# Hybrid encoder step on one core: another order and chaining of the 20 products of the down projection, later x tiles, later last h combinations

## The chip, the cores and the metric

The kernel runs on one core of one Trainium2 chip. The metric is the device time of one execution in microseconds (us), the median of several. Engines are named as in the profile: PE (TensorE matmul) and PEld (its weight loads), DVE (VectorE), ACT (ScalarE), POOL (GpSimd), SP (SyncE, which here only issues transfers).

## The reference

One step of a small streaming encoder with two layers, in float32, for 1024 prompt tokens and 8 x 16 sample tokens (1152 rows of 1024). Each layer is attention (a projection, banded attention, an output projection added to the residual x) and then an MLP, which is all that matters here:

```python
def mlp(x, g_norm, w_up, w_down):
    return jnp.square(jax.nn.relu(rmsnorm(x, g_norm) @ w_up)) @ w_down
...
        hp = hp + mlp(hp, g_mlp[layer], w_up[layer], w_down[layer])
        hs = hs + mlp(hs, g_mlp[layer], w_up[layer], w_down[layer])
```

`w_up` is 1024 x 4096, `w_down` 4096 x 1024. The second product, h @ w_down added to x, is called "down" below, the first "up".

## The kernel before, in words

**Stages.** For each of the two layers the kernel runs attention, the output projection, up (`mlp_up`) and down (`mlp_down`). x lives in memory as nine tiles of 128 tokens: 0 to 7 are the prompt and ST (8) is the sample. Every float32 operand of a matmul is split in a high and a low part (ACT casts, line 128; DVE subtracts, line 134), and every product of tiles is three matmuls (`mm3`, lines 746 to 748).

**Down as 20 products.** One pass covers half of the 4096 hidden columns, and there are two passes per layer (s = 0, 1). In a pass the h matrix is cut in 3 token thirds by 4 blocks, the weights in 4 blocks by 2 column halves, and the output x in 3 thirds (`PARTS`: which three x tiles form each third) by 2 column halves, six output pieces. Instead of 24 block products there are 20 (`RANK`), each of one combination of h blocks with one combination of weight blocks (`W_FORMS`, one or two blocks each: 4 of the 20 have one, 16 have two). `OUT_FORMS` says to which of the six pieces, with which sign, a product is added. A layer thus has 40 products, which I number 0 to 39 in the order in which they run.

**Chains.** `CHAINS` holds that order. The products of one chain accumulate in the same three PSUM banks (one per x tile of a third). After a product, DVE adds a bank to the x tiles wherever the form of this product differs from that of the next of the chain (line 1119, a "read": one for each differing piece and bank). A read inside a chain must be done before PE comes back to that bank in the next product; after the end of a chain the next one takes other banks. A negative number in `CHAINS` is a product of the other sign, made by swapping the two weight blocks, or, for those in `NEG_H`, by storing the negated h combination.

**What a product needs.** The h combination of a product is loaded from memory into one of three tiles a0 to a2 (`load_h`, line 1031, 768 KB) and split in place. The weight blocks are loaded once per pass into raw tiles r0 to r10 (`load_w`, 1 MB each, places by `RAW_AT`); for a form of two blocks DVE first adds or subtracts them (line 1067, here an "add"); the result is split into one of two tiles w0, w1. In the loop over products, iteration n loads the weights of product n + 3 (`AHEAD`), splits those of n + 1, adds those of n + 2, issues the matmuls and the reads of n, and then loads the h combination of the next product whose tile is free.

**One queue.** All these loads are issued by SP, and `load` chains each behind the one before, so their order on SP is the order of the program: a load that has to wait keeps back all that come after it. The x tiles are loaded on the same chain. `X_AT` says ahead of which product's h combination a third is loaded (three tiles of 512 KB): thirds 2, 1 and 0 with products 0, 1 and 3. `DOWN_HOME` lists the places of the tiles in SBUF from left to right. They lie over what up used: x5, x6, x7, the bias tiles, r4 and r5 lie over up's output tiles h, and so can be loaded only when these are read out.

**The h combinations.** Up works in 16 blocks of 256 hidden columns. After each pair of blocks DVE forms the combinations (`forms_even`, five transfers and two operations; `forms_odd`, 16 operations L935 to L968 of 128 x 384, mostly in place, and 15 transfers), and POOL stores each to memory (`form_store`, line 911, 192 KB). `COLS` says which third of an h tile is meant by which block row; it goes together with `PARTS`. The last pair of blocks feeds the second pass of down alone.

**The order on the engines** is made when the program is built: a scheduler walks the instructions by priority (program order, moved by `high_priority`) and by a model of when each can run; each engine then runs its own list strictly in order.

Of the kernel before, what the change touches and what calls it, by code (L numbers as in the profile page):

```python
# [8 lines left out]
F32 = mybir.dt.float32  # L9
# [7 lines left out]
P = 128  # L17
# [3 lines left out]
ST = NT  # L21
# [7 lines left out]
NFB = FF // FB  # L29
SIDE = (0, 1, 6, 2, 3, 4, 5)  # L30
RANK = 20
PARTS = ((5, 6, 7), (ST, 0, 1), (2, 3, 4))
COLS = (2, 0, 1)
W_FORMS = (
    "+.......", ".......+", "+......-", ".+.....+", ".....+..",
    "..+..-..", "..+.....", "...+.+..", "..+.+...", "+.....+.",
# [7 lines left out]
    "....+.", "..+.-.", "+.+...", "...-.+", "..+.-.",  # L44
)
CHAINS = (
    ((4,), (0, 10), (14, 15), (-13, 18), (12, 1, 2, 17, 9, 8), (-6, 5, 11, 3, 7), (16, 19)),
    ((0,), (-4, 15), (-14, 10), (-13, 18), (19, 16), (12, 1, 2, 17), (-6, 5, 11, 7, 3), (9, 8)),
)
NEG_H = ((6,), (6, 4))  # L50
RAW_AT = ((0, 7, 2, 8, 1, 6, 9, 3), (10, 7, 6, 3, 5, 4, 9, 8))
EPS = 1e-6
BIG = 1e30
NREL = 257
# [40 lines left out]
class Build:  # L95
# [682 lines left out]
    def mlp_up(self, layer, sx, x8, rp, raw0):  # L778
        nc = self.nc
        tt = nc.vector.tensor_tensor  # L780
        with ExitStack() as st:
# [9 lines left out]
            hp = self.pool(st, f"uh{layer}")  # L791

            def weights(b):
                raw = self.up_raw(layer, rp, b) if b else raw0
                quad = []
                for h in range(2):
                    q = [
                        take(f"q{b % 2}{v}") if h else rp[0].tile([P, 4, FB], F32R, tag=f"q{v}", name="wq")
                        for v in range(2)
                    ]  # L800
                    self.split(q[0], q[1], raw[h])
                    quad.append(q)
                b11, b12 = raw[0][:, :, 0:P], raw[0][:, :, P:FB]
                b21, b22 = raw[1][:, :, 0:P], raw[1][:, :, P:FB]
                t = b11, b22, b12, b21
                tt(t[0], b12, b11, ALU.subtract)
                tt(t[2], b22, b12, ALU.subtract)
                tt(t[1], b22, t[0], ALU.subtract)
                tt(t[3], b21, t[1], ALU.subtract)
                ts = [None] * 4  # L810
                for n in (1, 2, 0, 3):
                    w = take(f"t{b % 2}{n}")
                    self.split(w[:, 0], w[:, 1], t[n])
                    ts[n] = w[:, 0], w[:, 1]
                q = lambda h, n: [quad[h][v][:, :, n * P : n * P + P] for v in range(2)]
                return quad, [q(0, 0), q(1, 0), q(1, 1), ts[3], ts[0], ts[1], ts[2]]
# [79 lines left out]
            for b in range(NFB):  # L896
                quad, ws = weights(b)
                eh = [hp.tile([P, 3 * 3 * P], F32, tag="h", name="h", bufs=7) for _ in range(2)]
                if b == 0:
                    tokens(eh, quad, ws, slice(0, 256), False)  # L900
                    tokens(eh, quad, ws, slice(256, 512), True)
                else:
                    tokens(eh, quad, ws, slice(0, 512), True)
                if b % 2 == 0:
                    even = eh
                    self.forms_even(b // 2, eh)
                else:
                    self.forms_odd(b // 2, even + eh, hp.tile([P, 3 * 3 * P], F32, tag="h", name="ht", bufs=7))

    def form_store(self, c):  # L910
        return lambda p, z: self.nc.gpsimd.dma_start(self.hd[c // 4][:, p, c % 4], z)  # L911
# [1 line left out]
    def form_cut(self, t):  # L913
        return [t[:, COLS[i] * 3 * P : (COLS[i] + 1) * 3 * P] for i in range(3)]

# [12 lines left out]
    def forms_odd(self, c, eh, extra):  # L928
        tt, put = self.nc.vector.tensor_tensor, self.form_store(c)
        add, sub = ALU.add, ALU.subtract  # L930
        (a0, s10, a8), (a1, a5, s11), (a2, a6, a10), (a3, a7, a11) = map(self.form_cut, eh)
        u, w, z = self.form_cut(extra)
        put(16, a6)
        put(8, a2)
        tt(a8, a6, a8, add)  # L935
        put(14, a8)
        tt(a10, a6, a10, add)
        put(15, a10)
        tt(u, a8, s10, sub)
        if c < 4:  # L940
            tt(w, a10, a8, sub)
        else:
            tt(w, a8, a10, sub)
        tt(z, a1, a2, sub)
        tt(a1, a1, s11, sub)
        put(7, a1)
        put(19, a11)
        tt(a7, a7, a11, add)
        put(17, a7)
        tt(a5, a5, a11, sub)  # L950
        put(12, a5)
        tt(a2, z, s11, sub)
        put(5, a2)
        if c < 4:
            tt(w, a2, w, add)
        else:
            tt(w, w, a2, sub)
        put(4, w)
        tt(z, a5, z, sub)
        put(6, z)  # L960
        tt(a6, a0, a3, sub)
        tt(a6, a6, a5, sub)
        put(1, a6)
        tt(a3, a3, a7, sub)
        put(9, a3)
        tt(a0, a0, a3, sub)
        put(2, a0)
        tt(u, a0, u, add)  # L968
        put(0, u)

    def mlp_down(self, layer, out):
# [3 lines left out]
        with ExitStack() as st:  # L975
# [11 lines left out]
            def take(tag):  # L987
                return slots.pop(tag) if tag in slots else fresh(tag)
# [38 lines left out]
            def slot(n):  # L1027
                return 1 + n % 2 if n >= total - TAIL else n % 3

            def load(dst, src):  # L1030
                a = nc.sync.dma_start(dst, src)
                if self.sp is not None:
                    self.behind(self.sp, a)
                self.sp = a

            def load_w(n):
                s, p, g, *_, raws = seq[n]
                for r, f in enumerate(W_FORMS[p]):
                    if f != "." and r not in raws:
                        raws[r] = take(f"r{RAW_AT[s][r]}")  # L1040
                        l, h = divmod(r, 2)
                        load(raws[r], wd[l // 2, l % 2][:, 4 * s : 4 * s + 4, N[h]])

            def load_h(n):
                s, p, *_ = seq[n]
                aa[n] = take(f"a{slot(n)}")
                load(aa[n][:, 1].bitcast(F32), self.hd[s][:, p])
# [3 lines left out]
            def add_w(n):  # L1051
                if n >= total:
                    return
                s, p, g, *_, raws = seq[n]
                used = [(r, f) for r, f in enumerate(W_FORMS[p]) if f != "."]
                g = g if p not in NEG_H[s] else 1
                x, y = (raws[used[i][0]] for i in (0, -1))
                if len(used) == 1:
                    assert g == 1
                    src[n] = x  # L1060
                    return
                src[n] = x if n >= total - TAIL + 2 else take(f"s{n % 2}")
                plus = used[1][1] == "+"
                assert g == 1 or not plus
                if g < 0:
                    x, y = y, x
                tt(src[n], x, y, ALU.add if plus else ALU.subtract)  # L1067

            def split_w(n):
                if n >= total:  # L1070
                    return
                w = ws[n] = take(f"w{n % 2}")
                self.split(w[:, 0], w[:, 1], src.pop(n))
                a = aa[n]
                self.split(a[:, 0], a[:, 1], a[:, 1].bitcast(F32))
# [3 lines left out]
            def early(n):  # L1079
                return self.tc.high_priority(EARLY[n]) if n < len(EARLY) else nullcontext()  # L1080

            def load_x(i):
                for t in PARTS[i]:
                    load(xs[t], self.xd[t])

            for n in range(AHEAD):
                with early(n):
                    load_w(n)
                    load_h(n)
                if n in X_AT:  # L1090
                    load_x(X_AT[n])
            add_w(0)
            split_w(0)
            add_w(1)
            for n, (s, p, g, first, final, reads, _) in enumerate(seq):
                if layer == 0 and n == RANK:
                    self.prep_bias(self.dp)
                if n + AHEAD < total:
                    load_w(n + AHEAD)
                if n + AHEAD in X_AT:  # L1100
                    load_x(X_AT[n + AHEAD])
                split_w(n + 1)
# [4 lines left out]
                for i in range(3):  # L1107
# [9 lines left out]
                    for o, v in reads:  # L1117
                        x = xs[PARTS[o // 2][i]][:, N[o % 2]]
                        tt(x, x, banks[i], ALU.add if v > 0 else ALU.subtract)  # L1119
                    for part in {o // 2 for o, _ in reads}:  # L1120
                        if last[part] == n:
                            t = PARTS[part][i]
                            nc.sync.dma_start(out(t), xs[t])
# [634 lines left out]
def make_plan(tail, second):  # L1758
# [16 lines left out]
AFTER = mybir.DependencyInfo(mybir.DependencyClass.NoSync, mybir.DependencyReason.DATA)  # L1775
EARLY = (300, 150, 110, 90)
DOWN_HOME = (
    "s0", "s1", "r0", "r1", "r2", "r3", "x5", "x6", "x7", "bias", "r4", "r5", "+384", "x2", "x3", "x0", "+640",
    "a0", "x4", "x1", "x8", "r6", "a1", "a2", "w0", "w1", "r7", "r8", "r9", "r10",
)  # L1780
TAIL = 6
AHEAD = 3
X_AT = {0: 2, 1: 1, 3: 0}
WO_ORDER = [[0, 4, 1, 5, 2, 6, 7, 3, ST], [0, 4, 1, 5, 6, 2, 7, 3, ST]]

CFG = [
# [49 lines left out]
```

## Time and profile before

| | |
|---|---|
| median of 3 runs | 2397.39 us (2394.85 to 2402.23) |
| the profiled execution, its own time | 2401.58 us |
| its span, first to last instruction | 2399.8 us, so 1.8 us lie around it |
| granted TensorE clock, mean | 0.988 |
| busy: DVE, ACT, POOL | 1787.2 us (74%), 1272.6 us (53%), 573.2 us (24%) |
| down of layer 0, first to last matmul | 805.3 to 1167 us |
| down of layer 1 | 2045.1 to 2395.4 us |

Every row of a timeline has the start, the duration, the engine, the line, the operation, out<-in and a count; in brackets stands how long the engine had been idle and who released it. In a table by windows each engine's busy time is followed by its count of instructions, and PEclk is the granted clock as a share of full speed.

### The profile page before, as it was taken

What the parts mean: (1) busy time and instruction counts of PE and PEld (TensorE: products, weight loads), DVE (VectorE), ACT (ScalarE), POOL (GpSimd) and SP (SyncE); (2) the same over time, 40 slices, a digit from 0 to 9 for tenths busy, and PEclk for the clock granted to TensorE, in tenths of its full rate; (3) what the DMA queues carried; (4) which work ended last, traced back from release to release, by engine and by line L of the source; (5) the groups of instructions that cost most, each with busy time, mean ns of one, the idle gap of its engine ahead of it and who ended that gap; (6) DMA issues with size and microseconds to landing.
All of it is one profiled execution on the core that took longest, in us unless ns stands there. A gap on an engine that the chain in (4) does not pass through costs nothing.

```text
span 2399.8 us, 33255 instructions
## 1 busy us (share of the span) xinstructions
PE 2291.6 (95%) x11429; PEld 1903.1 (79%) x11429; DVE 1787.2 (74%) x3192; ACT 1272.6 (53%) x2503; POOL 573.2 (24%) x892
## 2 busy tenths in 40 slices
PE   7998999899999889999999999998999999899998
PEld 6787877788888668877778788886888888688877
DVE  6788786666566689899567876887665664898995
ACT  3777674555555334444267666665555555344432
POOL 4334332222222100001233444444122321100000
PEclk9999999999999999999999999999999999999999
DMA  7335545244343672535543655555343444734533
GB/s 254 119 109 167 170 149 201 87 135 143 127 141 120 253 244 93 206 132 182 181 152 113 197 162 170 172 165 166 96 142 118 157 140 148 276 110 139 199 102 122
DMA packets 216377, 375.38 MB, mean 156 GB/s; under 512 B 51144, under 2 KB 125840, under 8 KB 216208
## 3 DMA queue, kind: packets, MB, share of 16 engines
q1 hardware_dynamic: 193136, 300.89, 38.9%
q0 software_dynamic: 21776, 67.65, 7.7%
q10 hardware_dynamic: 1296, 4.72, 0.5%
q8 instruction: 90, 1.47, 0.3%
q14 instruction: 79, 0.65, 0.1%
HBM read 241.23 MB, written 130.90 MB: 155 GB/s over the span
## 4 chain that ended last, share of the span: by engine, by line
PE 68%; DVE 14%; DMA 8%; issue 4%; ACT 3%; POOL 1%; SPq 1%; ACTq 0%; DVEq 0%; POOLq 0%
PE ps_x L746 5%; PE ps_x L748 5%; PE ps_x L747 5%; PE ps_c L748 5%; PE ps_c L746 5%; PE ps_c L747 5%; PE ps_mm L219 4%; PE ps_mm L217 4%; PE ps_mm L218 4%; PE ps_y L748 2%; PE ps_y L747 2%; PE ps_y L746 2%; DVE w L134 2%; PE ps_tr L324 2%; DVE x L1119 2%
## 5 line engine op out<-in xcount | busy, mean ns | idle before, releaser
L746 PE MATMUL ps_c<-w,a 128*128 128x512 f32 x960 | 380.3, 396 | 29.7 <-ACT a L128 15.9
L747 PE MATMUL ps_c<-w,a 128*128 128x512 f32 x960 | 378.9, 395 | 5.2 <-DVE w L134 5.2
L748 PE MATMUL ps_c<-w,a 128*128 128x512 f32 x960 | 378.8, 395 | 4.7 <-DVE a L134 4.5
L911 POOL DMA_DIRECT2D hd<-h x272 | 147.2, 541 | 600.6 <-ACT h L820 263.1
L128 ACT CAST a<-a 128x1536 fp32r<-128x1536 f32 x80 | 118.6, 1482 | 242.5 <-DMA a<-hd 240.1
L746 PEld LDWEIGHTS ps_c<-w,a 128*128 128x128 f32 x960 | 183.0, 191 | 75.5 <-ACT a L128 18.0
L748 PEld LDWEIGHTS ps_c<-w,a 128*128 128x128 f32 x960 | 182.8, 190 | 46.9 <-DVE a L134 8.5
L747 PEld LDWEIGHTS ps_c<-w,a 128*128 128x128 f32 x960 | 182.9, 191 | 44.0 <-DVE w L134 6.6
L1119 DVE TENSOR_TENSOR x<-x,ps_c 128x512 f32<-128x512 f32 x246 | 161.0, 679 | 31.8 <-PE ps_c L748 31.6
L134 DVE TENSOR_TENSOR a<-a 128x1536 fp32r<-128x1536 f32 x80 | 140.4, 1755 | 56.0 <-ACT a L128 56.0
L217 PE MATMUL ps_mm<-w,hh 128*128 128x512 f32 x432 | 173.2, 402 | 6.4 <-POOL w L185 2.1
L128 ACT CAST w<-s 128x2048 fp32r<-128x2048 f32 x56 | 107.2, 1914 | 126.7 <-PE ps_c L748 119.0
L219 PE MATMUL ps_mm<-w,hl 128*128 128x512 f32 x432 | 172.6, 401 | 0.8 <-DMA hl<-hTd 0.6
L218 PE MATMUL ps_mm<-w,hh 128*128 128x512 f32 x432 | 171.7, 398 | 1.6 <-DVE w L190 1.6
L746 PE MATMUL ps_x<-sx,w 128*128 128x512 f32 (+1 forms) x408 | 158.4, 388 | 3.7 <-ACT h L867 2.7
L747 PE MATMUL ps_x<-sx,w 128*128 128x512 f32 (+1 forms) x408 | 154.8, 379 | 0.0
L748 PE MATMUL ps_x<-sx,w 128*128 128x512 f32 (+1 forms) x408 | 154.8, 379 | 0.0
L128 ACT CAST w<-ru 128x512 fp32r<-128x512 f32 (+1 forms) x160 | 110.0, 708 | 84.4 <-PE ps_y L747 32.0
L134 DVE TENSOR_TENSOR ptl<-ps_tr,pth 128x512 fp32r<-128x512 f32 x180 | 122.4, 685 | 24.3 <-ACT pth L128 19.2
L134 DVE TENSOR_TENSOR w<-s,w 128x2048 fp32r<-128x2048 f32 x56 | 127.9, 2284 | 15.5 <-ACT w L128 15.5
L134 DVE TENSOR_TENSOR w<-ru,w 128x512 fp32r<-128x512 f32 (+1 forms) x160 | 126.7, 794 | 15.1 <-ACT w L128 15.0
L1067 DVE TENSOR_TENSOR s<-r,r 128x2048 f32<-128x2048 f32 x56 | 127.7, 2284 | 2.8 <-DMA r<-in_w_down 2.8
(280 smaller groups left out, 5903.3 us busy)
## 6 DMA issues: line engine op xcount, KB each, us to landing
a<-hd SPq DMA_DIRECT2D x80, 768.0 KB, 4.2
hd<-h POOLq DMA_DIRECT2D x272, 192.0 KB, 2.5
ru<-in_w_up SPq DMA_DIRECT2D x64, 512.0 KB, 3.9
r<-in_w_down SPq DMA_DIRECT2D x32, 1024.0 KB, 8.0
x<-xd SPq DMA_DIRECT2D x41, 512.0 KB, 6.3
o<-oTd SPq DMA_DIRECT2D x52, 256.0 KB, 4.3
xd<-xo SPq DMA_DIRECT2D x18, 512.0 KB, 2.8
xo<-xd SPq DMA_DIRECT2D x18, 512.0 KB, 3.9
```

The costliest lines, as they stand in the source:

```text
L128: a = nc.scalar.copy(hi, src)
L134: return a, e.tensor_tensor(lo, src, hi.bitcast(F32), ALU.subtract)
L217: nc.tensor.matmul(ps, a, w[:, 0, k, :], start=(k == 0), stop=False)
L218: nc.tensor.matmul(ps, a, w[:, 1, k, :], start=False, stop=False)
L219: self.lp = nc.tensor.matmul(ps, b, w[:, 0, k, :], start=False, stop=(k == KC - 1))
L324: self.lp = nc.tensor.transpose(pt[:, i, :], get(i), self.ident)
L746: a = mm(ps, ah, bh, start=first, stop=False, skip_group_check=True)
L747: mm(ps, ah, bl, start=False, stop=False, skip_group_check=True)
L748: return a, mm(ps, al, bh, start=False, stop=last, skip_group_check=True)
L911: return lambda p, z: self.nc.gpsimd.dma_start(self.hd[c // 4][:, p, c % 4], z)
L1067: tt(src[n], x, y, ALU.add if plus else ALU.subtract)
L1119: tt(x, x, banks[i], ALU.add if v > 0 else ALU.subtract)
```

## The change

1. `CHAINS`, `NEG_H`: other orders and groupings of the 20 products in both passes. `RAW_AT`: other places of the raw weights.
2. `PARTS`, `COLS`, `DOWN_HOME`: the thirds (2, 3, 4) and (ST, 0, 1) change roles, and with them the names of the places; third 0 stays (5, 6, 7).
3. `X_AT`: third 0 is loaded ahead of product 5's h combination, no longer ahead of product 3's.
4. `forms_odd` of the last pair of blocks runs under a priority lowered by 400.
5. Inside `forms_odd` the signs follow the new `NEG_H`, and one operation reads another input. There are 16 operations and 15 transfers as before.

```diff
-PARTS = ((5, 6, 7), (ST, 0, 1), (2, 3, 4))
-COLS = (2, 0, 1)
+PARTS = ((5, 6, 7), (2, 3, 4), (ST, 0, 1))
+COLS = (2, 1, 0)
...
 CHAINS = (
-    ((4,), (0, 10), (14, 15), (-13, 18), (12, 1, 2, 17, 9, 8), (-6, 5, 11, 3, 7), (16, 19)),
-    ((0,), (-4, 15), (-14, 10), (-13, 18), (19, 16), (12, 1, 2, 17), (-6, 5, 11, 7, 3), (9, 8)),
+    ((-4, 15), (0, 10), (-6, 5, 11, 7, 3), (12, 1, 2, 17, 8, 9), (14,), (-13, 18), (19, 16)),
+    ((19, 16), (14, 15), (4,), (18, -13), (11, 5, -6, -12, -1, -2, 0, 10), (17, 9, 8), (3, 7)),
 )
-NEG_H = ((6,), (6, 4))
-RAW_AT = ((0, 7, 2, 8, 1, 6, 9, 3), (10, 7, 6, 3, 5, 4, 9, 8))
+NEG_H = ((4, 6), (6, 12, 1))
+RAW_AT = ((1, 3, 2, 7, 0, 6, 9, 8), (5, 3, 10, 6, 7, 8, 4, 9))
...
-                    self.forms_odd(b // 2, even + eh, hp.tile([P, 3 * 3 * P], F32, tag="h", name="ht", bufs=7))
+                    with self.tc.high_priority(-LATER) if b == NFB - 1 else nullcontext():
+                        self.forms_odd(b // 2, even + eh, hp.tile([P, 3 * 3 * P], F32, tag="h", name="ht", bufs=7))
...
-        tt(z, a1, a2, sub)
+        swap = lambda z, x, y, late: tt(z, y, x, sub) if late else tt(z, x, y, sub)
+        swap(w, a8, a10, c > 3)
+        swap(z, a1, a2, c > 3)
         tt(a1, a1, s11, sub)
...
-        tt(a2, z, s11, sub)
+        tt(a2, a1, a2, sub)
...
 DOWN_HOME = (
-    "s0", "s1", "r0", "r1", "r2", "r3", "x5", "x6", "x7", "bias", "r4", "r5", "+384", "x2", "x3", "x0", "+640",
-    "a0", "x4", "x1", "x8", "r6", "a1", "a2", "w0", "w1", "r7", "r8", "r9", "r10",
+    "s0", "s1", "r0", "r1", "r2", "r3", "x5", "x6", "x7", "bias", "r4", "r5", "+384", "x8", "x0", "x2", "+640",
+    "a0", "x1", "x3", "x4", "r6", "a1", "a2", "w0", "w1", "r7", "r8", "r9", "r10",
 )
 TAIL = 6
+LATER = 400
 AHEAD = 3
-X_AT = {0: 2, 1: 1, 3: 0}
+X_AT = {0: 2, 1: 1, 5: 0}
```

More of the change, by code (lines that the diff above doesn't have):

```diff
@@ L939, in forms_odd @@
         tt(u, a8, s10, sub)
[L940 to L943, printed above, removed]
-        tt(z, a1, a2, sub)
+        swap = lambda z, x, y, late: tt(z, y, x, sub) if late else tt(z, x, y, sub)
+        swap(w, a8, a10, c > 3)
+        swap(z, a1, a2, c > 3)
         tt(a1, a1, s11, sub)
@@ L949, in forms_odd @@
         put(17, a7)
-        tt(a5, a5, a11, sub)
+        swap(a5, a5, a11, c > 3)
         put(12, a5)
-        tt(a2, z, s11, sub)
+        tt(a2, a1, a2, sub)
         put(5, a2)
[L954 to L957, printed above, removed]
+        tt(w, w, a2, sub if c < 4 else add)
         put(4, w)
-        tt(z, a5, z, sub)
+        swap(z, a5, z, c > 3)
         put(6, z)
-        tt(a6, a0, a3, sub)
+        swap(a6, a0, a3, c > 3)
         tt(a6, a6, a5, sub)
```

## The prediction

> **What bounds the kernel now.** I read the busy table first, then the windows of down, then PE's waits there, then the queue behind the longest one.
>
> ```profile
> PE 2291.6 (95%) x11429; PEld 1903.1 (79%) x11429; DVE 1787.2 (74%) x3192; ACT 1272.6 (53%) x2503; POOL 573.2 (24%) x892
> ```
>
> PE is busy for 95% of the span, and the change takes away no matmul: 40 products per layer before and after. It can only touch stretches in which PE waits or has a lower clock. The next rows are windows of down for its matmuls alone (PE, PEld and DVE busy, then the granted clock).
>
> ```profile
> 805.30:836.00 30.70, 26.76 (x108) 21.17 (x107) 7.65 (x12) 0.94 0.52 198
> 836.00:842.50 6.50, 0.00 (x0) 0.00 (x0) 0.19 (x1) 0.81 0.98 341
> 842.50:855.00 12.50, 11.87 (x37) 9.05 (x38) 1.37 (x2) 0.69 0.80 304
> ...
> 969.00:1165.00 196.00, 188.86 (x812) 153.26 (x811) 45.79 (x71) 0.98 0.50 169
> ...
> 2081.10:2092.00 10.90, 10.29 (x36) 7.90 (x37) 0.68 (x1) 0.78 0.98 360
> ...
> 2148.00:2396.00 248.00, 241.89 (x1059) 197.69 (x1057) 56.94 (x87) 1.00 0.41 137
> ```
>
> The loss sits at the start of down: 3.9 us, 6.5 us, then a stretch at clock 0.69. Later it is thin: 7.1 us in 196, 6.1 us in 248. PE's own rows say what it waited for, layer 0 first and layer 1 below the dots:
>
> ```profile
> 805.28 0.39 PE L746 MATMUL ps_c<-w,a 128*128 128x512 f32 x1
> 822.93 0.47 PE L746 MATMUL ps_c<-w,a 128*128 128x512 f32 x1 [1.17 <-DVE x L1119]
> 825.63 0.50 PE L747 MATMUL ps_c<-w,a 128*128 128x512 f32 x1 [2.24 <-DVE w L134]
> 842.55 0.79 PE L746 MATMUL ps_c<-w,a 128*128 128x512 f32 x1 [7.09 <-ACT a L128]
> 844.35 0.80 PE L748 MATMUL ps_c<-w,a 128*128 128x512 f32 x1 [0.57 <-DVE a L134]
> ...
> 2045.12 0.39 PE L746 MATMUL ps_c<-w,a 128*128 128x512 f32 x1
> 2062.76 0.47 PE L746 MATMUL ps_c<-w,a 128*128 128x512 f32 x1 [1.17 <-DVE x L1119]
> 2065.47 0.80 PE L747 MATMUL ps_c<-w,a 128*128 128x512 f32 x1 [2.23 <-DVE w L134]
> 2081.14 0.80 PE L746 MATMUL ps_c<-w,a 128*128 128x512 f32 x1 [5.87 <-ACT a L128]
> ```
>
> PE waits twice on DVE, then 7.09 and 5.87 us for an h combination. Why that one is late stands on the SP queue (a row of the waits table, the queue's own rows, the last of them in layer 1) and on POOL:
>
> ```profile
> SPq L1031 <- DMA hd<-ht: 30.4, 1, 30.4
> ```
>
> ```profile
> 801.97 31.84 SPq L1031 DMA_DIRECT2D x<-xd  x3
> ...
> 832.98 0.83 SPq L1031 DMA_DIRECT2D x<-xd  x2
> 834.21 0.32 SPq L1031 DMA_DIRECT2D a<-hd  x1
> ...
> 2073.59 0.36 SPq L1031 DMA_DIRECT2D a<-hd  x1
> ```
>
> ```profile
> 830.66 0.54 POOL L911 DMA_DIRECT2D hd<-ht  x1 [2.46 <-DVE ht L968]
> ```
>
> The three x tiles of third 0 are one group from 801.97; a narrower window shows that two of them went only at 832.98. They wait until the last combination is stored, and the h load of product 3 waits behind them until 834.21. That store hangs on DVE, which has no room in that time:
>
> ```profile
> 797.00:831.00 34.00, 33.14 (x37) 0.95 0.66 256
> ```
>
> ```profile
> 815.63 2.28 DVE L1067 TENSOR_TENSOR s<-r,r 128x2048 f32<-128x2048 f32 x1
> 817.83 1.28 DVE L1119 TENSOR_TENSOR x<-x,ps_c 128x512 f32<-128x512 f32 x2
> ...
> 820.43 1.75 DVE L134 TENSOR_TENSOR a<-a 128x1536 fp32r<-128x1536 f32 x1
> 822.10 1.28 DVE L1119 TENSOR_TENSOR x<-x,ps_c 128x512 f32<-128x512 f32 x2
> 823.30 2.28 DVE L134 TENSOR_TENSOR w<-s,w 128x2048 fp32r<-128x2048 f32 x1
> 825.50 0.55 DVE L966 TENSOR_TENSOR h<-h 128x384 f32<-128x384 f32 x1
> 825.97 0.55 DVE L957 TENSOR_TENSOR ht<-ht,h 128x384 f32<-128x384 f32 x1
> ...
> 829.71 0.55 DVE L968 TENSOR_TENSOR ht<-h,ht 128x384 f32<-128x384 f32 x1
> ...
> 2069.55 0.54 DVE L968 TENSOR_TENSOR ht<-h,ht 128x384 f32<-128x384 f32 x1
> ```
>
> From start to start an add takes 2.20 us, a split of h 1.67, a split of weights 2.20, a read 0.60, a combination 0.47.
>
> **What the start costs now.** Matmuls at full clock follow each other by (2395.03 - 2391.63) / 15 = 0.227 us, so a product of 36 takes 8.16 us:
>
> ```profile
> 2391.63 0.39 PE L748 MATMUL ps_c<-w,a 128*128 128x512 f32 x1
> ...
> 2395.03 0.39 PE L748 MATMUL ps_c<-w,a 128*128 128x512 f32 x1
> ```
>
> Product 3 is due at 805.28 + 3 x 8.16 = 829.8 and starts at 842.55, 12.8 us late. The 0.57 us follow, and the clock of 0.69 over 12.5 us takes 0.31 x 12.5 = 3.9, with that wait partly inside, say 3.7. Layer 0: 17.0 us. In layer 1, product 3 is due at 2069.6 and starts 11.5 us late; the clock takes 0.22 x 10.9 = 2.4. Layer 1: 13.9 us. Together **30.9 us**.
>
> **The change part by part.** *X_AT* puts the third-0 loads behind the h loads of products 3 and 4, so the late stores no longer hold these back. Next in the queue is the h load of product 5, then a weight block for product 6; in layer 0 the bias transfers share the queue too. Product 5 is due 40.8 us after product 0, at 846.1 and 2085.9. From the end of the last combination to PE's start it took 842.55 - 830.25 = 12.3 us in layer 0 and 2081.14 - 2070.09 = 11.1 in layer 1, and the same steps stand in between (store, x tiles, h load, two splits). So nothing is lost if the last combination ends by 833.8 (2074.8 in layer 1); each us after that is a us of waiting.
>
> *Lowered priority and order.* When does the last combination end? The 16 operations and the 123 reads of a layer remain (41 per bank by the forms of either order, times three banks), and so do the 32 adds. Between 797.2 and 829.8 DVE must do, ahead of the combinations, four splits of each kind (15.5 us), adds for products 1 and 3 (4.4), two operations of up (1.2) and eight reads of products 0 to 2 (4.8): 25.9 of 32.6. The combinations need 16 x 0.47 = 7.5 of the 6.7 that are left. If they keep their turn they end as now, near 830. If they strictly come last, the next product leaves only 8.16 - (3.87 + 2.20 + 1.80) = 0.3 us, and they end at 838 to 842, when DVE runs dry. Put behind everything up to product 5, 849. I take 837, near the strict case: idle moments between the splits will take most of them earlier. Then product 5 is ready at 837 + 12.3 = 849.3, 3.2 us late; in layer 1, 239.8 later and with 11.1, 2.0 us late. Add the 0.6 after each, and the clock:
>
> ```profile
> 1147.15 0.75 PE L746 MATMUL ps_c<-w,a 128*128 128x512 f32 x1 [2.05 <-ACT a L128]
> ```
>
> ```profile
> 1150.00:1152.00 2.00, 2.00 (x6) 1.62 (x5) 0.00 (x0) 0.50 0.00 0
> ```
>
> Here a wait of 2.05 us was followed by clock 0.50, so I charge 2 us per layer. What remains is 3.2 + 2.0 + 1.2 + 4 = 10.4, and the start gains 30.9 - 10.4 = **20.5 us**. [...]
>
> *Third 0 read earlier*, by product 4 instead of 8.
>
> ```profile
> x<-xd SPq DMA_DIRECT2D x41, 512.0 KB, 6.3
> ```
>
> Released at 837 + 2.7 and landing 6.3 later, x6 is there at 846; its bank is full at 843.4. DVE stands 2.6 us at that read, with the split of product 5 behind it, whose h tile is later still. Cost 0, at most 2.6 per layer.
>
> *Reads in the chains.* Six-read products inside a chain are 7 and 29 now, 9, 29 and 30 afterwards. What product 29 costs product 30 is this, layer 0 and layer 1:
>
> ```profile
> 1079.10 0.50 PE L746 MATMUL ps_c<-w,a 128*128 128x512 f32 x1 [2.00 <-DVE x L1119]
> ...
> 2312.66 0.50 PE L746 MATMUL ps_c<-w,a 128*128 128x512 f32 x1 [2.01 <-DVE x L1119]
> ```
>
> One more such place is 0 to 2 us per layer. I take **+4.0** for both; the one-block products 29, 31 and 33 beside it lighten DVE, so up to 4 may come back.
>
> *At no cost.* Places: each load in its order keeps its place, under another name. r1 instead of r7 for product 2 may come sooner, but its h tile decides. ST, 0 and 1 are out after product 30 instead of 32; layer 1's start comes after PE's last product either way. Signs and the new input in the combinations: same count. If these covers fail, 2 us either way.
>
> **Sum.** 20.5 - 4.0 = 16.5 us. The profiled execution has 2401.58 us (span 2399.8 and 1.8 around it) and would have 2385.1; it lies 4.2 above the median of the runs, 2397.39, from which I get **2381 us**.
>
> **Rivals.** *Full recovery:* the combinations are done by 833.8, also if the priority moves nothing and they stay at 830. For: 6.7 us of room against 7.5. Against: full DVE. 30.9 - 4.0 = 26.9, **2370.5**.
>
> *The same stop, later:* they end at 841. Layer 0 waits 7.2 + 0.6 + 3.7, layer 1 6.0 + 0.6 + 2.4: 20.5 of 30.9 remains; less 4.0, **2391**.
>
> *Slower:* they end at 849, behind the work up to product 5. For: the lowered priority covers several products. Against: the reads of x6 cannot be served before, so DVE's list must hold them sooner. 15.2 + 0.6 + 3.7 and 14 + 0.6 + 2.4 make 36.5, with the 4.0 a loss of 9.6, **2407**. It decides from 844: there 26.5 remain, and each us later adds 2.
>
> **How the numbers follow.** Forecast 0.42, full recovery 0.22, same stop 0.18, slower 0.18. A measurement here tells about 0.3%, 7.2 us, from no change: faster ends at 2390.2, slower begins at 2404.6. A third of the same-stop case counts as faster: 0.42 + 0.22 + 0.06 = 0.70; 0.04 of the slower case stays under the bound: same 0.16, slower 0.14. The range leaves out about a tenth at each end: the lower part of full recovery, with the reads' 4 us given back (2366), and the upper half of the slower case (2406).
>
> **What would show it.** Right: SP issues the h loads of products 3 and 4 ahead of the third-0 x tiles; no wait at product 3; L968 ends near 837; a wait of 2 to 4 us at product 5; product 30 or 31 waiting for reads. Wrong: L968 ending before 834 or after 842, an h load held back by the bias transfers, or DVE standing at the reads of product 4.

## The result, and the profile after

| | before | after |
|---|---|---|
| median | 2396.68 us (2394.85 to 2402.23, 4 runs) | 2369.84 us (2365.98 to 2374.17, 4 runs) |
| ratio, 95% interval | | 0.9885 [0.9861, 0.9908] |
| profiled execution, its span | 2401.58, 2399.8 us | 2365.98, 2364.2 us |
| granted TensorE clock, mean | 0.988 | 0.995 |
| down, first to last matmul, layer 0 and 1 | 361.8, 349.9 us | 343.2, 337.7 us |

The change made the kernel 26.8 us faster; the interval of the ratio leaves 22 to 33. By the profiled executions down became 18.6 + 12.2 = 30.8 us shorter. (Down is read here from starts given to 0.1 us, so a difference of two is good to about 0.2.) That it equals the 30.9 us put on the start is partly chance. From product 0 to product 6 it now takes 51.5 and 51.0 us where it took 66.0 and 65.0, which is 28.5 less; products 6 to 19 take 4.4 us less, nearly all in layer 0; and from product 20 to the last matmul it takes 2.0 us more. The rest of the span, in which the edits change next to nothing, differs by 4.8 us (1688.1 and 1683.3). That is no effect of the change: two executions of one and the same program differ by 7.5 us there (the run e3 below). So I compare ratios of medians, and in the profiles down alone.

In after.py the lines have moved: a read is line 1115 (was 1119), an add 1063 (1067), a load 1027 (1031), a store of a combination 912 (911), and the last combination is that of line 953.

PE is still the bound, with the same 11429 matmuls and 15 us less of busy time. This is the page's busy table:

```profile
PE 2276.7 (96%) x11429; PEld 1891.4 (80%) x11429; DVE 1783.0 (75%) x3192; ACT 1274.2 (54%) x2503; POOL 574.4 (24%) x892
```

The windows of down for its matmuls alone (PE, PEld and DVE busy, then the granted clock, the DMA share and GB/s), cut at the same distances from product 0 as before where both have them:

```profile
802.70:833.40 30.70, 30.25 (x131) 24.43 (x131) 5.91 (x9) 1.00 0.92 357
833.40:840.00 6.60, 6.47 (x29) 5.03 (x28) 1.86 (x3) 1.00 0.82 297
840.00:852.40 12.40, 11.61 (x51) 9.27 (x50) 2.60 (x4) 1.00 0.44 152
...
966.40:1145.30 178.90, 170.99 (x736) 138.04 (x735) 44.37 (x68) 0.99 0.45 155
...
2124.70:2359.80 235.10, 228.30 (x996) 185.51 (x994) 56.57 (x87) 1.00 0.41 138
```

The stretch of 6.5 us with no matmul has 29 of them now, and the clock stays at 1.00 where it was 0.94, 0.81 and 0.69. PE's own rows, layer 0 and then layer 1, show all of its waits in the first six products that are over 0.3 us:

```profile
802.73 0.39 PE L746 MATMUL ps_c<-w,a 128*128 128x512 f32 x1
...
828.30 0.50 PE L747 MATMUL ps_c<-w,a 128*128 128x512 f32 x1 [0.36 <-DVE w L134]
...
848.62 0.50 PE L746 MATMUL ps_c<-w,a 128*128 128x512 f32 x1 [0.79 <-DVE x L1115]
...
2047.28 0.50 PE L747 MATMUL ps_c<-w,a 128*128 128x512 f32 x1 [0.39 <-DVE w L134]
...
2067.15 0.50 PE L746 MATMUL ps_c<-w,a 128*128 128x512 f32 x1 [0.77 <-DVE x L1115]
```

Up to product 3 alone there were 11.1 and 9.8 us of waits, and the lower clock after them (0.69 and 0.78). Now there are 1.15 and 1.16 us in six products. The SP queue shows why:

```profile
811.09 0.32 SPq L1027 DMA_DIRECT2D a<-hd  x1
...
819.58 0.32 SPq L1027 DMA_DIRECT2D a<-hd  x1
820.03 8.47 SPq L1027 DMA_DIRECT2D x<-xd  x3
828.62 0.36 SPq L1027 DMA_DIRECT2D a<-hd  x1
```

The h loads of products 3 and 4 are issued at 811.09 and 819.58, then come the x tiles of third 0. They wait for the stores as before, but they stand for only 8.47 us instead of 31.84, and the h load of product 5 behind them goes at 828.62, in good time. In the waits table the queue's wait for the stores, 30.4 us before, is this row:

```profile
SPq L1027 <- DMA hd<-ht: 7.1, 1, 7.1
```

And the end of the last combination on DVE, with the split of the weights of product 2 and the add for product 3 ahead of it:

```profile
816.08 2.29 DVE L134 TENSOR_TENSOR w<-r,w 128x2048 fp32r<-128x2048 f32 x1
...
818.88 2.29 DVE L1063 TENSOR_TENSOR s<-r,r 128x2048 f32<-128x2048 f32 x1
...
823.22 0.56 DVE L953 TENSOR_TENSOR ht<-ht,h 128x384 f32<-128x384 f32 x1
```

It ends at 823.78, which is 21.05 us after product 0. Before it ended 830.25 - 805.28 = 24.97 us after it; the prediction had 31.7.

### The profile page after: what moved, and what is told of

Read it like the earlier page. It is cut to its first block, busy times and chain, and to the rows that moved or that the text cites. A ratio compares the mean times of both kernels' runs of the same rounds, so it can differ in the third digit from the quotient of the medians.

```text
span 2364.2 us, 33257 instructions
## 1 busy us (share of the span) xinstructions
PE 2276.7 (96%) x11429; PEld 1891.4 (80%) x11429; DVE 1783.0 (75%) x3192; ACT 1274.2 (54%) x2503; POOL 574.4 (24%) x892
## 4 chain that ended last, share of the span: by engine, by line
PE 66%; DVE 14%; DMA 11%; ACT 4%; issue 3%; POOL 1%; SPq 1%; DVEq 0%; ACTq 0%; POOLq 0%
PE ps_c L748 5%; PE ps_x L746 5%; PE ps_c L746 5%; PE ps_c L747 5%; PE ps_x L748 5%; PE ps_x L747 5%; PE ps_mm L217 3%; DMA r<-in_w_down 3%; PE ps_mm L219 3%; PE ps_mm L218 3%; DVE w L134 2%; PE ps_y L748 2%; PE ps_y L747 2%; PE ps_y L746 2%; PE ps_tr L324 2%
## 5 line engine op out<-in xcount | busy, mean ns | idle before, releaser
L746 PE MATMUL ps_c<-w,a 128*128 128x512 f32 x960 | 376.1, 392 | 9.1 <-DVE x L1115 8.2
L747 PE MATMUL ps_c<-w,a 128*128 128x512 f32 x960 | 375.5, 391 | 6.0 <-DVE w L134 5.9
L748 PE MATMUL ps_c<-w,a 128*128 128x512 f32 x960 | 374.9, 391 | 3.3 <-DVE a L134 3.2
L746 PEld LDWEIGHTS ps_c<-w,a 128*128 128x128 f32 x960 | 180.6, 188 | 53.4 <-issue 5.1
L747 PEld LDWEIGHTS ps_c<-w,a 128*128 128x128 f32 x960 | 180.6, 188 | 46.6 <-DVE w L134 9.9
L748 PEld LDWEIGHTS ps_c<-w,a 128*128 128x128 f32 x960 | 180.6, 188 | 42.3 <-DVE a L134 5.1
```

The costliest lines, as they stand in the source:

```text
L746: a = mm(ps, ah, bh, start=first, stop=False, skip_group_check=True)
L747: mm(ps, ah, bl, start=False, stop=False, skip_group_check=True)
L748: return a, mm(ps, al, bh, start=False, stop=last, skip_group_check=True)
```

## The experiments

**The theories.** Theory Q (the queue): the loss came from SP, where the h load of product 3 stood behind x tiles that waited for the last combinations; X_AT alone takes it away, as long as the combinations end within 28.5 us of product 0. The rivals are these: the order of the products gives the gain by taking work off DVE; the lowered priority does something, for or against; and what is not X_AT costs something that the gain hides. "Down" is the sum of both layers in the profiled execution, 711.7 us before and 680.9 after.

| run | median, us | ratio, 95% interval | down, us |
|---|---|---|---|
| after | 2369.84 | 0.9885 [0.9861, 0.9908] | 680.9 |
| e1_queue_undone | 2396.36 | 0.998 [0.997, 0.999] | 702.6 |
| e2_queue_alone | 2380.01 | 0.9914 [0.99, 0.9927] | 691.7 |
| e3_priority_undone | 2373.59 | 0.9886 [0.9872, 0.99] | 681.7 |
| e4_old_pass1 | 2375.5 | 0.989 [0.9872, 0.9907] | 682.7 |
| e5_old_pass0 | 2392.05 | 0.9967 [0.9955, 0.9979] | 699.6 |
| e6_queue_and_thirds | 2387.16 | 0.9946 [0.9931, 0.9962] | 697.0 |
| e7_more16 | 2413.84 | 1.0049 [1.0034, 1.0064] | 724.1 |
| e8_more32 | 2434.44 | 1.014 [1.0124, 1.0155] | 745.3 |
| e9_ten_first | 2376.73 | 0.9903 [0.9889, 0.9916] | 690.4 |
| e10_homes | 2407.8 | 1.0032 [1.0019, 1.0045] | 695.0 |
| e11_old_thirds | 2375.36 | 0.9898 [0.9883, 0.9913] | 683.2 |

### The queue undone: all of the change but X_AT

```diff
-X_AT = {0: 2, 1: 1, 5: 0}
+X_AT = {0: 2, 1: 1, 3: 0}
```

> The changed kernel, with only the place of the third-0 x loads put back (X_AT 3: 0). Theory Q (the queue): these loads stand ahead of the h load of product 3 again and wait there for the last store. The last combination now ends 21.1 us after the start of product 0 (823.8 against 802.7), and 12.3 us lie between it and the start of the product, so product 3 can start at 33.4 us where it is due at 24.5 to 25: a wait of 8 to 9 us there in layer 0, 7 to 8 in layer 1, with 0.6 and some 2 to 3.5 us of low clock behind each: 20 to 25 us slower than the changed kernel, most of the gain gone. Theory C (the chains): the new order alone ends the combinations early enough and evens out the reads, and the place of the loads is worth little: under 8 us slower, with no wait over 3 us at product 3.

Nearly the whole gain is gone: 0.998. SP's rows in layer 0, and PE's waits at product 3 of both layers:

```profile
802.74 24.12 SPq L1027 DMA_DIRECT2D x<-xd  x3
...
826.99 0.35 SPq L1027 DMA_DIRECT2D a<-hd  x1
```

```profile
835.53 0.80 PE L746 MATMUL ps_c<-w,a 128*128 128x512 f32 x1 [8.62 <-ACT a L128]
...
2067.71 0.80 PE L746 MATMUL ps_c<-w,a 128*128 128x512 f32 x1 [7.27 <-ACT a L128]
```

The x tiles stand for 24.12 us again, and the h load behind them goes at 826.99, 8.5 us ahead of PE's start. The combinations end early, as in the changed kernel (21.0 us after product 0), and the waits at product 2 are gone too. All of that, without X_AT, buys 0.2%.

### The queue alone: X_AT in the kernel before

```diff
-X_AT = {0: 2, 1: 1, 3: 0}
+X_AT = {0: 2, 1: 1, 5: 0}
```

> The kernel before, with only the third-0 x loads moved to product 5 (X_AT 5: 0). Theory Q: the waits of 7.1 and 5.9 us with the 0.6 and the 3.7 and 2.4 us of low clock go, the two waits on DVE (1.2 and 2.2 us) stay: 20 us faster than before, 16 to 22. Theory C: with the old order the last combination ends 25 us after product 0, the h load of product 5 is held back in its turn, and at most 8 us are gained.

0.9914, or 20.6 us of 2397, about the 20 that Q gave. PE's waits at product 2, and the last combination:

```profile
820.57 0.47 PE L746 MATMUL ps_c<-w,a 128*128 128x512 f32 x1 [1.17 <-DVE x L1119]
...
823.28 0.50 PE L747 MATMUL ps_c<-w,a 128*128 128x512 f32 x1 [2.24 <-DVE w L134]
```

```profile
831.21 0.56 DVE L968 TENSOR_TENSOR ht<-h,ht 128x384 f32<-128x384 f32 x1
```

In the first six products no long wait is left, only 0.62 us at product 4, but the two waits on DVE at product 2 are there, each as long as in the kernel before. The combinations end 28.9 us after product 0 (802.9), 3.9 us later than in the kernel before, although the order of the products is the same: with the loads at another place the build puts one split of h and one add more ahead of that end in DVE's list. That is just behind the bound of 28.5, and it costs nothing, because the waits at product 2 let product 5 start only 47.2 us after product 0 instead of 40.8. What after has beyond this, 0.9885 against 0.9914 and 10.8 us of down, must come from the rest of the change.

### The priority undone

```diff
-                    with self.tc.high_priority(-LATER) if b == NFB - 1 else nullcontext():
+                    with nullcontext():
```

> The changed kernel with the lowered priority of the last combinations taken out. Theory P (the priority frees DVE at the start of down): the combinations move ahead of splits and reads again, the two waits of 1.2 and 2.2 us return, 5 to 9 us slower. Rival (the priority moves nothing, since each of these operations is taken when its inputs are ready): the same rows, the same waits, within 3 us of the changed kernel.

The same as after, 0.9886. More than that: the two programs have the same list of instructions on every engine, and so have those built with LATER = 0, 4000 and -400. Here the lowered priority changes nothing. The two profiles of this one program differ by 0.8 us in down and by 7.5 in the rest of the span, so a single profile tells no smaller difference.

### The second pass alone undone

This is after with the old second pass (its CHAINS, NEG_H, RAW_AT, and the signs in `forms_odd` that go with them).

```diff
-    ((19, 16), (14, 15), (4,), (18, -13), (11, 5, -6, -12, -1, -2, 0, 10), (17, 9, 8), (3, 7)),
+    ((0,), (-4, 15), (-14, 10), (-13, 18), (19, 16), (12, 1, 2, 17), (-6, 5, 11, 7, 3), (9, 8)),
...
-NEG_H = ((4, 6), (6, 12, 1))
+NEG_H = ((4, 6), (6, 4))
```

> The changed kernel with the second pass of each layer in the old order and chains (its signs and raw places with it); the first pass stays new. My step on the reads (one more six-read product inside a chain costs up to 2 us per layer): 0 to 4 us faster than the changed kernel. Rival (the long chain with its one-block products is the lighter one): 0 to 5 us slower, with waits on reads after products 29 and 33 as before the change.

0.989, within 0.1% of after and of e3, and down is 1.8 and 1.0 us longer. The new second pass neither gains nor costs anything that this can tell; with intervals of 0.0014 and 0.0018 that leaves some 5 us either way.

### The first pass alone undone

The same for the first pass.

```diff
-    ((-4, 15), (0, 10), (-6, 5, 11, 7, 3), (12, 1, 2, 17, 8, 9), (14,), (-13, 18), (19, 16)),
+    ((4,), (0, 10), (14, 15), (-13, 18), (12, 1, 2, 17, 9, 8), (-6, 5, 11, 3, 7), (16, 19)),
...
-NEG_H = ((4, 6), (6, 12, 1))
+NEG_H = ((6,), (6, 12, 1))
```

> The changed kernel with the first pass of each layer in the old order and chains (its signs and raw places with it); second pass, x places and queue stay new. Theory F (the order of the first pass is what is left of the gain): the waits of 1.2 us on a read and 2.2 us on a weight split in products 2 and 3 return in both layers, with a little low clock: 5 to 8 us slower than the changed kernel, about the time of the queue edit alone (2380). Rival (the swapped thirds, not the chains, make the combinations ready sooner): within 2 us of the changed kernel.

The expectation of 5 to 8 us was a miss: it is 0.0081 or 19 us slower than e3, and down is 17.9 us longer. DVE's last combination, then SP:

```profile
839.49 0.56 DVE L964 TENSOR_TENSOR ht<-h,ht 128x384 f32<-128x384 f32 x1
```

```profile
823.33 20.21 SPq L1027 DMA_DIRECT2D x<-xd  x3
843.64 1.36 SPq L1027 DMA_DIRECT2D a<-hd  x2
```

The combinations end 34.8 us after product 0 (805.2), behind the bound, not at 28.9 as with the same chains in e2. So the x tiles stop the queue again, for 20.21 us, now ahead of product 5. The larger part of PE's waiting is not from this stop, though. PE's two waits at product 2 are back, on a read (1.64 us) and on the split of the weights, 3.87 us together in layer 0 and 3.88 in layer 1. At product 5 there is one of 2.00 us in each layer. Layer 0:

```profile
826.01 0.79 PE L747 MATMUL ps_c<-w,a 128*128 128x512 f32 x1 [2.23 <-DVE w L134]
...
855.22 0.50 PE L748 MATMUL ps_c<-w,a 128*128 128x512 f32 x1 [2.00 <-DVE a L134]
```

What differs from e2 are the thirds and the second pass; the next run looks at the thirds.

### The thirds exchanged, with the old order

This is e2 with PARTS, COLS and DOWN_HOME as changed.

```diff
-PARTS = ((5, 6, 7), (ST, 0, 1), (2, 3, 4))
-COLS = (2, 0, 1)
+PARTS = ((5, 6, 7), (2, 3, 4), (ST, 0, 1))
+COLS = (2, 1, 0)
```

> The kernel before with the third-0 loads at product 5 and the swapped thirds (the tuples of token thirds, their columns and their places); both passes in the old order. My step that the swap costs and brings nothing: within 2 us of the queue edit alone, 2378 to 2382. Rival (the swap makes the last combinations ready sooner): 4 to 7 us faster than that, and the last combination ends 21 us after product 0 instead of 29.

A miss again: not the same as e2 but 0.0032 or 7.7 us slower. The last combination:

```profile
834.84 0.55 DVE L968 TENSOR_TENSOR ht<-h,ht 128x384 f32<-128x384 f32 x1
```

The combinations end 32.1 us after product 0 (803.3). With the old order, then, the exchange delays them by some 3 us: two combinations, one split of h and one read more stand between product 0 and their end in DVE's list, by the times per operation 3.2 us. Why the build orders them so I have not settled. The late end is not what this run pays for, since product 5 has no wait over 0.3 us. The waits that grew are those on the split of the weights at product 2 (3.18 and 3.17 us, from 2.24) and on a read at product 8 of layer 0 (4.58, from 1.75).

### More work for the last combinations

After, with one pair of operations of the last block repeated, nine times in e7 and seventeen in e8 (16 and 32 operations more in each layer, which write the same values again).

```diff
-        swap(a6, a0, a3, c > 3)
-        tt(a6, a6, a5, sub)
+        for _ in range(9 if c == 7 else 1):
+            swap(a6, a0, a3, c > 3)
+            tt(a6, a6, a5, sub)
```

> The changed kernel with 16 repeated operations in the last combinations of each layer (the pair of operations that makes the combination of product 1 is done nine times; the result is the same). They take 7.5 us of DVE and end the last combination at 29 to 31 us after product 0, where my bound for a free start of product 5 is 28.5. By my price (nothing up to the bound, a us for each us behind it): 0 to 8 us slower than the changed kernel over both layers, the wait at product 5 at most 2.5 us. Rival (DVE has no room at the start of down, so each us that it gets more is a us of PE): 15 us slower, spread over products 1 to 5 as waits on splits and reads.

> The same with 32 repeated operations per layer (15 us of DVE). By my price the last combination ends at 36 to 42 us, 8 to 13 us behind the bound, and product 5 waits so long for its h combination (released by ACT), with 0.6 us and 2.4 to 3.7 us of low clock behind it: 22 to 34 us slower than the changed kernel, as slow as before the change or slower. Rival (DVE alone): 30 us slower too, but as waits on splits and reads from product 1 on, without one long wait at product 5.

These measure the price of a late end. The last combination and PE's wait at product 5, in layer 0 of e7:

```profile
850.11 0.56 DVE L965 TENSOR_TENSOR ht<-h,ht 128x384 f32<-128x384 f32 x1
```

```profile
862.38 0.80 PE L746 MATMUL ps_c<-w,a 128*128 128x512 f32 x1 [14.82 <-ACT a L128]
```

and of e8:

```profile
859.51 0.56 DVE L965 TENSOR_TENSOR ht<-h,ht 128x384 f32<-128x384 f32 x1
```

```profile
872.50 0.80 PE L746 MATMUL ps_c<-w,a 128*128 128x512 f32 x1 [24.98 <-ACT a L128]
```

PE starts 862.38 - 850.67 = 11.7 us after the end in e7 and 872.50 - 860.07 = 12.4 in e8; the prediction had 12.3 for this path. In layer 1 it is 13.6 and 14.0, where the prediction had 11.1. From e7 to e8 the end moves by 9.4 us in layer 0 and the wait by 10.2: about one us of waiting for each us behind the bound. The two layers together then cost 0.0091 or 21.8 us more. So the price held, but both expectations missed the times. e7 was to wait at most 2.5 us and e8 8 to 13; they waited 14.82 and 24.98 us in layer 0, and are some 39 and 61 us slower than after by the ratios, not 0 to 8 and 22 to 34. What was wrong was how far work moves the end. Sixteen operations of 0.47 us are 7.5 us, and in e7 the end moved from 21.05 to 45.8 us after product 0, by 24.8: the operations of a pair write the same tile, each in turn, and in DVE's list splits, adds and reads of the next products stand between them. The sixteen more of e8 stand behind all that, one right after the other, at 0.59 us each, which makes the 9.4.

### A weight sum ahead of product 2 again

```diff
-    ((-4, 15), (0, 10), (-6, 5, 11, 7, 3), (12, 1, 2, 17, 8, 9), (14,), (-13, 18), (19, 16)),
+    ((-4, 15), (10, 0), (-6, 5, 11, 7, 3), (12, 1, 2, 17, 8, 9), (14,), (-13, 18), (19, 16)),
```

> The changed kernel with the second chain of the first pass turned round: (10, 0) in place of (0, 10). Product 10 has a weight form of two blocks and comes third now, so DVE has an add (2.2 us) before product 2 again, as in the kernel before; the reads stay. Theory W: in the kernel before it was this add, ahead of the split of the weights of product 2, that made PE wait 2.24 us there, and ahead of the last combination that made it end late. Then a wait of 1 to 2.3 us on the split weights comes back at product 2, in both layers, the last combination ends some 2 us later (about 23 us after product 0, from 21.05), still ahead of the bound of 28.5, so no wait at product 5; the time is 2 to 6 us longer than that of the changed kernel, ratio to the kernel before 0.990 to 0.9915. Rival: the reads alone made DVE late, and an add more is covered: no wait at product 2 and the time of the changed kernel, ratio 0.9885 within 0.001.

0.9903, 4.3 us more than after by the ratios; the intervals overlap, but down says it more sharply, 690.4 against 680.9, or 9.5 us. The edit does one thing more than the expectation said: with the product called 0 in `CHAINS` at the end of its chain there are three more reads per layer, after the fourth product (DVE has 3198 operations instead of 3192). PE's wait at product 2 in layer 0 (3.40 in layer 1), then DVE's rows at that place:

```profile
823.39 0.50 PE L747 MATMUL ps_c<-w,a 128*128 128x512 f32 x1 [3.48 <-DVE w L134]
```

```profile
814.11 2.28 DVE L1063 TENSOR_TENSOR s<-r,r 128x2048 f32<-128x2048 f32 x1
...
820.58 0.55 DVE L953 TENSOR_TENSOR ht<-ht,h 128x384 f32<-128x384 f32 x1
821.05 2.28 DVE L134 TENSOR_TENSOR w<-s,w 128x2048 fp32r<-128x2048 f32 x1
```

Theory W is right on the wait, which is even longer than 2.3 us, and wrong on the combinations: they end at 821.13, 18.2 us after product 0, earlier than in after, because here they stand ahead of the late split. The add delays the split of the weights of product 2 from 816.08 to 821.05. Down is that of e2 within 1.3 us. Up to product 6, where the wait at product 2 stands, e9 takes 6.8 us longer than after in the two layers together, and e2 8.4. So most of what after has beyond X_AT seems to be a product with a single weight block in third place. The three reads run after that wait, so the wait itself is not theirs; what else they cost I have not separated. Of the 9.5 us, 2.7 lie behind product 6.

### Third 0 moved off the combinations' tiles

```diff
-    "s0", "s1", "r0", "r1", "r2", "r3", "x5", "x6", "x7", "bias", "r4", "r5", "+384", "x2", "x3", "x0", "+640",
+    "s0", "s1", "r0", "x5", "x6", "x7", "r1", "r2", "r3", "bias", "r4", "r5", "+384", "x2", "x3", "x0", "+640",
```

> The kernel before with one line of places changed and nothing else: in DOWN_HOME x5, x6 and x7 change places with r1, r2 and r3, so that third 0 no longer lies over the tiles from which the last combinations are stored, and the raw weights r2 and r3 do. The order of the loads stays (X_AT is 0: 2, 1: 1, 3: 0). Theory Q, in its narrow form: what stopped the queue was not the place of the x loads in it but that these loads had to wait until the combinations were stored. Then the h load of product 3 follows the h load of product 2 without the 32 us, the long wait at product 3 (7.09 and 5.87 us) goes or shrinks to under 2, the waits of 1.17 and 2.24 before it stay, and the gain is that of the later x loads alone, 16 to 22 us: ratio 0.9908 to 0.9933. Rival: the raw weights that now lie over the tiles stop the same queue at an earlier or later place, and no more than 5 us are gained, ratio over 0.998.

As a time this went against the expectation, 0.3% slower instead of faster; in down it did as expected, 16.7 us shorter. SP's rows, with X_AT as in the kernel before:

```profile
801.21 2.58 SPq L1031 DMA_DIRECT2D x<-xd  x3
813.03 0.32 SPq L1031 DMA_DIRECT2D a<-hd  x1
...
821.56 12.51 SPq L1031 DMA_DIRECT2D r<-in_w_down  x2
834.47 0.34 SPq L1031 DMA_DIRECT2D a<-hd  x1
```

The same third-0 loads at the same place in the queue go through in 2.58 us instead of 31.84, so their place in the queue alone is no harm: what stopped the queue before was the memory that they load over. The raw weights that lie there now stop for 12.51 us, further back. PE's rows, the first at product 5, the second at the start of layer 1:

```profile
854.83 0.50 PE L747 MATMUL ps_c<-w,a 128*128 128x512 f32 x1 [3.89 <-DVE w L134]
...
1175.57 3.98 PE L210 MATMUL ps_n<-identr,x 128*128 128x128 f32 x16 [16.90 <-DMA x<-xd]
```

Product 3 has no wait now, product 5 has 3.89 us. The 21 us that make it slower lie outside: from the last matmul of layer 0 to product 0 of layer 1 it takes 899.0 us (1158.3 to 2057.3) instead of 878.0 (1167.1 to 2045.1), with a new wait of 16.90 us for layer 1's x tiles.

### The thirds in their old roles, with the new order

After with PARTS, COLS and the names in DOWN_HOME as before.

```diff
-PARTS = ((5, 6, 7), (2, 3, 4), (ST, 0, 1))
-COLS = (2, 1, 0)
+PARTS = ((5, 6, 7), (ST, 0, 1), (2, 3, 4))
+COLS = (2, 0, 1)
```

> The changed kernel with the thirds in their old roles: PARTS, COLS and the names in DOWN_HOME as in the kernel before, with orders, places of the weights and X_AT as changed. Theory N: the roles of the thirds cost nothing by themselves, ratio 0.9885 within 0.0015. Theory P: the exchange costs some 5 to 7 us by itself, as the run with the old orders suggested (7 us longer with the exchange); then this kernel is 4 to 7 us faster than the changed one, ratio 0.9855 to 0.987. Rival R: the new orders need the new roles, since the tiles of the third that is used first or last must be free or out at another time; then it is slower by 3 us or more, with a wait for an x tile at the start or a longer end.

0.9898 [0.9883, 0.9913], and 683.2 us of down against 680.9: some 3 us slower than after by the ratios, which the intervals do not tell from nothing. Theory P is wrong, since nothing got faster. The wait for an x tile that R expects at the start is not there. What the exchange costs in e6 it costs with the old order; with the new one it brings at most a few us.

## Why the prediction was right, and where it was wrong

**The forecast and what came.** The forecast was 2381 us, a gain of 16.5; it became 2369.84, a gain of 26.8. The direction and the cause were right, but the path by which the forecast got its number did not happen. By its own signs it is refuted: the last combination was to end near 837, and an end before 834 was to show it wrong.

**The bound and the cause: right.** The loss sits at the start of down, and most of the gain came there: 28.5 of 30.8 us by product 6. That it came from the queue is shown from three sides: X_AT alone brings 20.6 us (e2), the rest without X_AT 5 (e1), and with X_AT untouched the stop goes once the loads no longer lie over the combinations' tiles (e10, in down).

**X_AT: right.** The h loads of products 3 and 4 went ahead, product 3 has no wait worth naming, the bias transfers held nothing back, and the path of 12.3 us held in layer 0 of e7 and e8 (11.7 and 12.4). The bound of 28.5 is that of a product 5 that comes on time.

**Lowered priority and order: this step failed.** It took 837 for the end of the last combination, 31.7 us after product 0, and from it 10.4 us that would remain at product 5 of the two layers. It is 21.05 us, 7.4 inside the bound of 28.5, and no such wait exists. (The "239.8 later" of this step should read 1239.8; its 2.0 us follow from that.) Two things were wrong in it. The priority was taken at its word, and it changes no list (e3). And the order was counted as neutral for the start, because the totals of a layer are the same. They are, but not what stands ahead of the last combination. DVE's groups in the stretch from product 0 to that end are these before (the tenth read starts 0.07 us ahead of the end and lies behind it):

```profile
L1119 DVE TENSOR_TENSOR x<-x,ps_c 128x512 f32<-128x512 f32 x10 | 6.5, 678 | 0.0
L134 DVE TENSOR_TENSOR w<-s,w 128x2048 fp32r<-128x2048 f32 x2 | 4.6, 2282 | 0.0
...
L134 DVE TENSOR_TENSOR w<-r,w 128x2048 fp32r<-128x2048 f32 x1 | 2.3, 2283 | 0.0
```

and after:

```profile
L1115 DVE TENSOR_TENSOR x<-x,ps_c 128x512 f32<-128x512 f32 x6 | 3.9, 684 | 0.0
L134 DVE TENSOR_TENSOR w<-r,w 128x2048 fp32r<-128x2048 f32 x1 | 2.3, 2290 | 0.0
...
L134 DVE TENSOR_TENSOR w<-s,w 128x2048 fp32r<-128x2048 f32 x1 | 2.3, 2284 | 0.0
```

Three reads (1.8 us) and one split of weights (2.2) are gone from ahead of it: 4.0 us, and the end moved by 24.97 - 21.05 = 3.9. With X_AT at product 5 in both, the old order ends at 28.9 (e2), so there the new one brings 7.8. That earlier end was hardly needed by itself: in e2 PE does not wait for the late one. What the order gave beyond X_AT is at product 2. The wait of 2.24 us on the split of the weights went with the early split (e9). The wait of 1.17 us on a read is absent in after and in e9 alike, where product 2 opens a chain and so takes other banks. Behind these two waits the clock was at 0.50 (826.40 to 829.70 before). The prediction had all this inside its 30.9 but in no step of its own.

**Reads in the chains: not found.** The step had +4.0 us and a wait at product 30 or 31. PE's rows after show the waits at the starts of products 28 and 29:

```profile
1041.84 0.47 PE L746 MATMUL ps_c<-w,a 128*128 128x512 f32 x1 [2.15 <-DVE x L1115]
...
1051.38 0.47 PE L746 MATMUL ps_c<-w,a 128*128 128x512 f32 x1 [1.09 <-DVE x L1115]
```

They stand in for the 2.00 and 1.36 us at products 30 and 34 of the kernel before. From product 20 to the last matmul it takes 175.4 and 172.5 us, where it took 175.4 and 170.5: 2.0 more in all, and 1.9 more in e3. With the old second pass in the new kernel (e4) it is 0.7 longer than after, not shorter. So the cost lies between 0 and 2 by the traces, and e4 tells no more within its 5 us. That up to 4 might come back was in the text; the sum left it out.

**Third 0 read earlier, and what was costed at nothing: about right.** The price, 0.79 and 0.77 us of wait at product 5, lies inside the 0 to 2.6 given, but for another reason. The prediction let DVE stand at a read of product 4 until x6 has landed. DVE has no idle time there: the read starts at 847.90 because an add of 2.27 us runs from 845.70 ahead of it. The exchange of the thirds costs nothing that can be told here (e11) but does with the old order (e6), which nothing in the prediction saw.

**The case that came.** It is the rival of full recovery, 2370.5 us, "also if the priority moves nothing". Its condition is what the traces show, an end of the combinations well inside the bound; its reason, that they "stay at 830", is not, for they moved. That its time comes within 1 us is luck as well: it takes off 4.0 us for reads, of which at most 2 came, and it leaves out the 4.4 us of products 6 to 19, which no step had. Its chance of 0.22 was too low against 0.42, because the step above took what an edit says for what it does.

## What to carry to other kernels

A transfer that waited for memory to come free (31.84 us here) held up all that the same queue had behind it, so put first on a queue what can go first; look at the longest issue row of the queue and at what lies behind it. Ahead of a critical moment count the work that stands before it, not the totals of the stage: orders with equal totals moved the end of the same operations from 21 to 35 us (after and e5). Which product stands third mattered too: one whose weights need no sum saved the wait of 2.24 us at product 2. And before counting on a priority, compare the lists that are built with it and without it.

## What the runs showed of the hardware that was not expected

The clock did not follow the length of the wait. The prediction charged 2 us of half clock for each wait of about 2 us, from the wait of 2.05 us at 1147.15 with 0.50 behind it. After the wait of 2.15 us at 1041.84 the clock of the changed kernel stayed whole (1.00), and after that of 3.48 us in e9 it was halved for some 3 us. Windows of PE after the wait, in after and then in e9:

```profile
1041.80:1044.00 2.20, 2.16 (x10) 1.00 0.59 243
1044.00:1047.00 3.00, 3.00 (x15) 1.00 0.00 0
```

```profile
825.00:827.00 2.00, 2.00 (x6) 0.50 0.71 282
827.00:830.00 3.00, 3.00 (x13) 0.91 0.32 90
```

The run e3, the same program as after, shows that the length of the wait alone does not decide it. The same wait of 2.15 us stands at its product 28, and there the clock was halved, 0.50 over 3.3 us:

```profile
1044.58 0.77 PE L746 MATMUL ps_c<-w,a 128*128 128x512 f32 x1 [2.15 <-DVE x L1115]
```

```profile
1044.60:1047.90 3.30, 3.30 (x8) 0.50 0.37 155
```

So the 2 us for each such wait were an estimate that fits one execution of this program (0.50 after 2.15 us in e3) and not the other (1.00 after 2.15 us in after). What decides between the two was not shown.
